# Where the last projection's weight sums are made in a hybrid encoder block

## The chip, the cores and the metric

The kernel runs on one core of a Trainium2 chip. The metric is device time in microseconds (us), the median of several executions. Five engines have instruction queues of their own, and each works its queue in order: PE (TensorE, matrix products), DVE (VectorE), ACT (ScalarE), POOL (GpSimd) and SP (SyncE, which here only issues transfers, DMAs, between the main memory and the memory on the chip). They wait for one another by semaphores. PE writes into PSUM, a small memory of banks that DVE and ACT read out.

## The reference

One layer of a hybrid encoder over 512 frames of 1024 features, all in float32:

```
xn = rmsnorm(x);  u = xn @ w_in            # q | k | v | rnn_x | rnn_gate | gate_A | gate_B
ya = chunked_band_attention(q, k, v) @ w_attn_out
xc = causal_depthwise_conv(rnn_x)          # width 4
hr = rg_lru(xc, ...)                       # 16 diagonal gate blocks, then a scan over time
yb = (hr * gelu(rnn_gate)) @ w_rnn_out
h  = x + (sigmoid(gate_A) * ya + sigmoid(gate_B) * yb) @ w_o
g, up = split(rmsnorm(h) @ w_ffn_in)
out = rmsnorm(h + (silu(g) * up) @ w_ffn_out)
```

The last projection, `w_ffn_out`, has 2816 x 1024 weights. Eleven blocks of 256 rows make it up. Three of them (0, 1, 10) are multiplied plainly; the other eight form four units of two blocks, each multiplied by a Strassen-like scheme: 7 products in place of 8, of sums of the blocks. The sums of the weights (t1 to t4 of a unit) depend on nothing but the weights.

## The kernel before

Activations lie feature by feature or frame by frame in tiles of 128 partitions. Every float32 product is made of three reduced products (`mm3`, L76 to L78): operand and weight are split into a high part (ACT casts, L82) and a low part (DVE subtracts, L83). Weights come in halves of 512 KB: SP issues the load of a `raw` tile (three buffers), ACT and DVE split it into a `whl` tile (four buffers), PE reads that. `weights(name, ahead)` fetches ahead in a fixed list of chunks.

The stages that matter here, in the order of time:

1. The recurrent stage (about 37 to 163 us): a loop over j = 0, 2, 4, 6. For each of two columns c it projects `xr` and makes the convolution (`rnn_conv`: ACT, then three taps on DVE at L495, then the cast and split of `xch` on ACT and POOL), projects `gr` and makes GeLU of it on ACT and DVE, then makes the gates (`rnn_gates`: six small matmuls at L516 into the PSUM tile `rg`, of which there is one buffer, read by four ACT instructions at L520 and L521). From the gates come `u` and `a` (ACT L525 and L526 with the small vectors `sp2` and `spm4`, DVE L528 and L532, POOL L530). After each second j a square root on ACT (L554), then DVE's L537, the scan over time (L538), L539. Last the loop projects `gb`. Below, rg5, xc5 and so on stand for the tile of j = 5.
2. The recurrent way out: the values of the attention's first group (`v_tile(0, t)`), then `yb`, eight columns.
3. Attention, 16 heads, with other projections between; PE's order there is written out by hand.
4. The attention's way out: `ya`, eight columns, then `w_o`.
5. The feed-forward part and the last projection.

Where no order is written out, a scheduler sets the order of each engine's queue at build time, by its own estimate of when each instruction could start. `sp2` and `spm4` come from `softplus_neg` (L436 to L466), a chain of small DVE operations on the tile `sp_p` that the scheduler puts between others.

`spill(u, rooms)` makes the four sums of unit u: four loads of 512 KB from `w_ffn_out` into four buffers, four subtractions on DVE (L749 to L752, each reading the results of those ahead), four stores of 512 KB into a tile `sums` in main memory. The last stage loads the sums from there (L929). Before the change unit 0 is called ahead of `v_tile(0, 0)`, unit 1 at `yb` column 2, units 2 and 3 at `ya` columns 1 and 4. The rooms are tiles of attention (`pt`) and of the values (`v`) that are free at that time.

Of the kernel before, what the change touches and what calls it, by code (L numbers as in the profile page):

```python
# [8 lines left out]
F32 = mybir.dt.float32  # L9
# [5 lines left out]
P = 128  # L15
D = 1024
S = 512
# [19 lines left out]
def block_kernel(ctx: ExitStack, tc: tile.TileContext, x, norm_mix_g, w_in, b_merge, rel_table,  # L37
# [28 lines left out]
    dr = ctx.enter_context(tc.tile_pool(name="dr", bufs=1, space=bass.MemoryType.DRAM))  # L66
# [63 lines left out]
    front, units = (0, 1, 10), ((2, 3), (4, 5), (6, 7), (8, 9))  # L130
# [254 lines left out]
    _, xnT = features(xnp, "xn", "xnT")  # L385
# [189 lines left out]
    def gate(w, j):  # L575
        po = tile_of(f"g{'ab'[w]}{j - j % 2}", j % 2)
        act.activation((ta, zB)[w][j], po[:], AF.Tanh, bias=hb[:, 16 + 8 * w + j:17 + 8 * w + j], scale=0.5)

    conv = {}
    for j in range(0, KT, 2):  # L580
        for c in range(2):
            conv[j + c] = rnn_conv(j + c, tile_of(f"xr{j}", c, ahead=2))
        for c in range(2):
            po = tile_of(f"gr{j}", c, "mm" if j == 0 else "t")
            conv[j + c] += (rnn_gelu(j + c, po),)
            gates_of(j + c)
        for c in range(2):
            gate(1, j + c)
# [39 lines left out]

    q_tile(0)
    k_tile(0)  # L630
    rw2_stack.close()
    rw_stack.close()
    aw2_stack, aw2 = opened("aw2", 2)
    aw_stack, aw = opened("aw", 2, "right")
# [99 lines left out]
        for n in names.split():  # L734
            kinds[n[0]](int(n[1:]))

    sums_d = [[dr.tile([P, 2, S], F32, name=f"sums{u}_{n}") for n in range(4)] for u in range(len(units))]

    def fo_block(i, cc):
        rows = w_ffn_out[2 * P * i:2 * P * (i + 1), cc * S:(cc + 1) * S]  # L740
        return rows.rearrange("(k p) e -> p k e", p=P)

    def spill(u, rooms):

        r = [pl.tile([P, 2, S], F32, tag=tag, bufs=bufs, name=f"spill{u}_{n}") for n, (pl, tag, bufs) in enumerate(rooms)]
        for n in range(4):
            sp.dma_start(out=r[n][:], in_=fo_block(units[u][n // 2], n % 2))
        b11, b12, b21, b22 = (t[:] for t in r)
        dve.tensor_sub(b11, b12, b11)  # L749
        dve.tensor_sub(b12, b22, b12)  # L750
        dve.tensor_sub(b22, b22, b11)
        dve.tensor_sub(b21, b21, b22)  # L752
        for n, i in enumerate((0, 3, 1, 2)):
            sp.dma_start(out=sums_d[u][n][:], in_=r[i][:])

    spill(0, [(aw2, "pt", 4)] * 4)
    for t in range(NT):
        v_tile(0, t)

    for j in range(KT):  # L760
        if j == 6:
            prob = scores(0)
        if j == 2:
            spill(1, [(aw2, "pt", 4)] * 4)
        po = mm_tile(f"po_yb{j}")
        project(po, weights(f"yb{j - j % 2}"), j % 2, rnn)
        dve.scalar_tensor_tensor(zB[j], zB[j], 1.0, po[:], ALU.add, ALU.mult)
# [14 lines left out]

    _, mT = features(xnp, "xn", "mT")
    for j in range(KT):
        if j in (1, 4):
            spill(2 + j // 4, [(aw, "v", 8)] * 4)
        py = mm_tile(f"po_ya{j}")
        project(py, weights(f"ya{j - j % 2}"), j % 2, aT)
        dve.scalar_tensor_tensor(ta[j], ta[j], 1.0, py[:], ALU.add, ALU.mult)
        dve.tensor_add(ta[j], ta[j], zB[j])  # L790
        split_pair(mT[j], ta[j])
# [129 lines left out]
    rooms = [(wp, "whl", 4)]  # L921
# [19 lines left out]
    for j in range(2, FT, 2):  # L941
# [4 lines left out]
        g, u = (sc.tile([P, 4, 256], F32, tag=f"c{w}", name=f"c_{w}{j}") for w in "gu")  # L946
# [201 lines left out]
```

## Time and profile before

| what | us |
|---|---|
| median of 3 runs | 866.72 (866.55 to 866.92) |
| the profiled execution's own time | 866.45 |
| its span, first to last instruction | 864.6 |
| PE busy | 852.5 (99%) |
| DVE busy | 603.5 (70%) |
| ACT busy | 499.4 (58%) |
| POOL busy | 96.7 (11%) |

The granted clock of TensorE was 0.998 over the span. An engine's busy time is the sum of what it worked, not what it held up; a wait shows as idle time before an instruction, with the instruction that ended it. In the views each instruction has its line in the kernel, its engine, what it writes and reads, its shape, its start and its length; L82 is line 82. Matmuls overlap in the records: an instruction of 0.39 us starts every 0.22 to 0.23 us.

### The profile page before, as it was taken

What the parts mean: (1) busy time and instruction counts of PE and PEld (TensorE: products, weight loads), DVE (VectorE), ACT (ScalarE), POOL (GpSimd) and SP (SyncE); (2) the same over time, 40 slices, a digit from 0 to 9 for tenths busy, and PEclk for the clock granted to TensorE, in tenths of its full rate; (3) what the DMA queues carried; (4) which work ended last, traced back from release to release, by engine and by line L of the source; (5) the groups of instructions that cost most, each with busy time, mean ns of one, the idle gap of its engine ahead of it and who ended that gap; (6) DMA issues with size and microseconds to landing.
All of it is one profiled execution on the core that took longest, in us unless ns stands there. A gap on an engine that the chain in (4) does not pass through costs nothing.

```text
span 864.6 us, 12947 instructions
## 1 busy us (share of the span) xinstructions
PE 852.5 (99%) x4920; PEld 747.7 (86%) x4920; DVE 603.5 (70%) x929; ACT 499.4 (58%) x862; POOL 96.7 (11%) x135
## 2 busy tenths in 40 slices
PE   8999999999999999999999999999999999999996
PEld 6977887888888888888888889999999999988885
DVE  5786776674566656566568556888887887399973
ACT  7687687542366656576623365655655556374544
POOL 2022212210113313223200000000000001000011
PEclk9999999999999999999999999999999999999999
DMA  8223324585442213232197811433433333295602
GB/s 271 87 89 96 97 76 122 205 304 184 130 127 73 74 49 110 74 110 75 54 315 264 288 53 49 129 116 98 128 101 115 99 99 98 79 327 159 193 22 97
DMA packets 91901, 113.13 MB, mean 131 GB/s; under 512 B 6080, under 2 KB 71216, under 8 KB 91840
## 3 DMA queue, kind: packets, MB, share of 16 engines
q1 hardware_dynamic: 88160, 104.65, 37.8%
q10 hardware_dynamic: 3680, 7.67, 3.0%
q8 instruction: 38, 0.62, 0.3%
q14 instruction: 23, 0.19, 0.1%
HBM read 101.78 MB, written 10.53 MB: 130 GB/s over the span
## 4 chain that ended last, share of the span: by engine, by line
PE 97%; ACT 1%; DVE 1%; DMA 1%; issue 0%; SPq 0%; DVEq 0%; ACTq 0%
PE po_out L76 4%; PE po_out L77 4%; PE po_out L78 4%; PE p_fg L76 2%; PE o L711 2%; PE p_fg L78 2%; PE p_fu L78 2%; PE p_fg L77 2%; PE p_fu L77 2%; PE p_fu L76 2%; PE pT L691 2%; PE po_gb L77 2%; PE po_gb L76 2%; PE po_ga L76 2%; PE po_v L76 2%; PE po_ga L78 2%
## 5 line engine op out<-in xcount | busy, mean ns | idle before, releaser
L680 POOL TENSOR_SCALAR p<-p,rl 128x128 f32<-128x128 f32 (+1 forms) x64 | 39.6, 637 | 160.6 <-DVE rl L678 160.5
L677 ACT ACTIVATE p<-p,m 128x128 f32<-128x128 f32 (+1 forms) x64 | 35.8, 562 | 12.7 <-DVE m L676 12.7
L918 POOL TENSOR_TENSOR act_lo<-act,act_hi 128x1024 fp32r<-128x1024 f32 x1 | 2.4, 2412 | 298.6 <-ACT act_hi L917 298.6
L83 DVE TENSOR_TENSOR pp<-pT,pp 128x384 fp32r<-128x384 f32 (+1 forms) x48 | 27.8, 596 | 9.8 <-ACT pp L82 9.7
L83 DVE TENSOR_TENSOR whl_qk<-raw_qk,whl_qk 128x1024 fp32r<-128x1024 f32 x16 | 21.5, 1346 | 14.4 <-ACT whl_qk L82 14.3
L676 DVE CUSTOM_DVE_ANT_0 p<-s,bias 128x128 f32<-128x128 f32 (+1 forms) x64 | 29.2, 483 | 2.1 <-PE s L673 2.0
L83 DVE TENSOR_TENSOR whl_fg_s<-s_fg,whl_fg_s 128x1024 fp32r<-128x1024 f32 x20 | 25.6, 1291 | 5.0 <-ACT whl_fg_s L82 5.0
L76 PE MATMUL po_gr<-xnT,whl_gr 128*128 128x512 f32 (+1 forms) x80 | 28.1, 352 | 0.1
L77 PE MATMUL po_xr<-xnT,whl_xr 128*128 128x512 f32 (+1 forms) x80 | 27.9, 354 | 0.0
L77 PE MATMUL po_gr<-xnT,whl_gr 128*128 128x512 f32 (+1 forms) x80 | 27.8, 348 | 0.0
L83 DVE TENSOR_TENSOR whl_fu_s<-s_fu,whl_fu_s 128x1024 fp32r<-128x1024 f32 x20 | 24.0, 1221 | 5.1 <-ACT whl_fu_s L82 5.1
L78 PE MATMUL po_gr<-xnT,whl_gr 128*128 128x512 f32 (+1 forms) x80 | 27.5, 348 | 0.0
L78 PE MATMUL po_xr<-xnT,whl_xr 128*128 128x512 f32 (+1 forms) x80 | 27.3, 346 | 0.0
L76 PE MATMUL po_xr<-xnT,whl_xr 128*128 128x512 f32 (+1 forms) x80 | 26.6, 351 | 0.6 <-ACT xnT L363 0.6
L82 ACT ACTIVATE whl_fg_s<-s_fg 128x1024 fp32r<-128x1024 f32 x20 | 20.9, 1054 | 10.5 <-PE q_fg L78 5.5
L82 ACT ACTIVATE whl_qk<-raw_qk 128x1024 fp32r<-128x1024 f32 x16 | 16.8, 1051 | 16.2 <-PE po_yb L78 8.8
L76 PE MATMUL po_gb<-xnT,whl_gb 128*128 128x512 f32 x64 | 25.2, 393 | 0.3 <-DVE sp_p L455 0.3
L76 PE MATMUL po_ga<-xnT,whl_ga 128*128 128x512 f32 x64 | 25.3, 395 | 0.0
L77 PE MATMUL po_gb<-xnT,whl_gb 128*128 128x512 f32 x64 | 25.3, 395 | 0.0
L76 PE MATMUL po_q<-xnT,whl_qk 128*128 128x512 f32 x64 | 25.0, 391 | 0.0
L78 PE MATMUL po_ga<-xnT,whl_ga 128*128 128x512 f32 x64 | 25.0, 391 | 0.0
L76 PE MATMUL po_k<-xnT,whl_qk 128*128 128x512 f32 x64 | 25.0, 390 | 0.0
(380 smaller groups left out, 3213.4 us busy)
## 6 DMA issues: line engine op xcount, KB each, us to landing
raw_fg<-in_w_ffn_in_dram SPq DMA_DIRECT2D x24, 512.0 KB, 4.6
raw_fu<-in_w_ffn_in_dram SPq DMA_DIRECT2D x22, 512.0 KB, 4.0
raw_qk<-in_w_in_dram SPq DMA_DIRECT2D x32, 256.0 KB, 3.2
spill<-in_w_ffn_out_dram SPq DMA_DIRECT2D x16, 512.0 KB, 7.2
sums<-spill SPq DMA_DIRECT2D x16, 512.0 KB, 3.9
raw_t<-sums SPq DMA_DIRECT2D x16, 512.0 KB, 4.7
raw_b<-in_w_ffn_out_dram SPq DMA_DIRECT2D x12, 512.0 KB, 4.4
raw_xr<-in_w_in_dram SPq DMA_DIRECT2D x8, 512.0 KB, 4.7
```

What stands on the lines that cost most here:

```text
L76: pe.matmul(o, sh, mh, start=start, stop=False, skip_group_check=parts)
L77: pe.matmul(o, sh, ml, start=False, stop=False, skip_group_check=parts)
L78: pe.matmul(o, sl, mh, start=False, stop=stop, skip_group_check=parts)
L82: act.activation(hi, src, AF.Copy)
L83: dve.tensor_sub(lo, src, f(hi))
L676: dve.tensor_tensor_reduce(prob[qb][:], scs[qb], bias[:, S - w:S], -1.0, 3e38, ALU.add, ALU.min, nmax[:, qb:qb + 1])
L677: act.activation(prob[qb][:], prob[qb][:], AF.Exp, bias=nmax[:, qb:qb + 1], scale=-1.0, accum_out=lsum[:, qb:qb + 1])
L680: pool.tensor_scalar(prob[qb][:], prob[qb][:], rl[:, qb:qb + 1], 1.0, ALU.mult, ALU.mult)
L691: pe.transpose(pt[:, at * P:(at + 1) * P], prob[qb][:, kb * P:(kb + 1) * P], ident[:])
L711: pe.matmul(po[:, S - n:S], st, pp[i][:, part, lo:lo + n], start=kb == 0 and part == 0, stop=kb == NT - 1 and part == 1)
L918: (pool if i == 0 else dve).tensor_sub(lo[:], o[:], f(hi[:]))
```

## The change

The calls of `spill` are moved. Units 0, 1 and 2 are made in the recurrent stage, at the head of j = 2, 4 and 6, in four buffers of their own (a pool `early`, which is closed at the end of the stage). Unit 3 is made at `yb` column 3. No call is left in the attention's way out. The helpers move up in the file, so later lines have other numbers.

```diff
+    sums_d = [[dr.tile([P, 2, S], F32, name=f"sums{u}_{n}") for n in range(4)] for u in range(len(units))]
+    def spill(u, rooms):
+        r = [pl.tile([P, 2, S], F32, tag=tag, bufs=bufs, name=f"spill{u}_{n}") for n, (pl, tag, bufs) in enumerate(rooms)]
+        for n in range(4):
+            sp.dma_start(out=r[n][:], in_=fo_block(units[u][n // 2], n % 2))
+        b11, b12, b21, b22 = (t[:] for t in r)
+        dve.tensor_sub(b11, b12, b11)
+        dve.tensor_sub(b12, b22, b12)
+        dve.tensor_sub(b22, b22, b11)
+        dve.tensor_sub(b21, b21, b22)
+        for n, i in enumerate((0, 3, 1, 2)):
+            sp.dma_start(out=sums_d[u][n][:], in_=r[i][:])
+
+    early_stack, early = opened("early", 4)
+
     conv = {}
     for j in range(0, KT, 2):
+        if j >= 2:
+            spill(j // 2 - 1, [(early, "spill", 4)] * 4)
         for c in range(2):
             conv[j + c] = rnn_conv(j + c, tile_of(f"xr{j}", c, ahead=2))
...
     k_tile(0)
+    early_stack.close()
     rw2_stack.close()
...
-    spill(0, [(aw2, "pt", 4)] * 4)
     for t in range(NT):
         v_tile(0, t)
     for j in range(KT):
         if j == 6:
             prob = scores(0)
-        if j == 2:
-            spill(1, [(aw2, "pt", 4)] * 4)
+        if j == 3:
+            spill(3, [(aw2, "pt", 4)] * 4)
         po = mm_tile(f"po_yb{j}")
...
     for j in range(KT):
-        if j in (1, 4):
-            spill(2 + j // 4, [(aw, "v", 8)] * 4)
         py = mm_tile(f"po_ya{j}")
```

The scheduler spreads the new instructions over the stage: units 0 and 1 start in the queues beside the work of j = 0 and 1, so all three units stand between the first column's convolution and that of j = 4. Three places show it. Names end in the buffer's number.

The first is DVE's queue where `sp2` and `spm4` end. Before:

```order
L456 TENSOR_TENSOR sp_p_407<-sp_p_407,sp_s2_405 128x8
L457 TENSOR_SCALAR sp_p_407<-sp_p_407 128x8
L458 TENSOR_TENSOR sp_p_407<-sp_p_407,sp_s_403 128x8
L533 SCALAR_TENSOR_TENSOR gt0_1_556<-gt0_1_556,xc0_476 128x512
L461 SCALAR_TENSOR_TENSOR sp_n_424<-sp_p_407,sp_n_424 128x8
L463 TENSOR_SCALAR sp2_427<-sp_n_424 128x8
L465 TENSOR_SCALAR spm4_429<-sp_n_424 128x8
```

The same chain in the changed kernel:

```order
L456 TENSOR_TENSOR sp_p_407<-sp_p_407,sp_s2_405 128x8
L591 TENSOR_TENSOR spill1_0_997<-spill1_1_998,spill1_0_997 128x1024
L457 TENSOR_SCALAR sp_p_407<-sp_p_407 128x8
L458 TENSOR_TENSOR sp_p_407<-sp_p_407,sp_s_403 128x8
L461 SCALAR_TENSOR_TENSOR sp_n_424<-sp_p_407,sp_n_424 128x8
L463 TENSOR_SCALAR sp2_427<-sp_n_424 128x8
L465 TENSOR_SCALAR spm4_429<-sp_n_424 128x8
L533 SCALAR_TENSOR_TENSOR gt1_1_628<-gt1_1_628,xc1_527 128x512
L495 SCALAR_TENSOR_TENSOR xc2_775<-po_xr2_0_750,vc_383,xc2_775 128x511
```

The first subtraction of unit 1 (L591) has come into the chain, five rows ahead of `sp2`, and the first tap of xc2 now follows that chain.

The second is DVE's queue around the taps of xc4 and xc5. Before:

```order
L538 SCALAR_TENSOR_TENSOR u2_827<-a2_831,gt2_1_822 128x512
L538 SCALAR_TENSOR_TENSOR u2_827<-a3_884,gt3_1_876 128x512
L539 SCALAR_TENSOR_TENSOR u2_827<-u2_827,g2_806 128x512
L539 SCALAR_TENSOR_TENSOR u2_827<-u2_827,g3_860 128x512
L495 SCALAR_TENSOR_TENSOR xc4_1007<-po_xr4_0_982,vc_383,xc4_1007 128x511
L495 SCALAR_TENSOR_TENSOR xc4_1007<-po_xr4_0_982,vc_383,xc4_1007 128x510
L495 SCALAR_TENSOR_TENSOR xc4_1007<-po_xr4_0_982,vc_383,xc4_1007 128x509
L83 TENSOR_TENSOR whl_gb4_0_974<-raw_gb4_0_972,whl_gb4_0_974 128x1024
L83 TENSOR_TENSOR whl_gb4_4_979<-raw_gb4_4_977,whl_gb4_4_979 128x1024
L495 SCALAR_TENSOR_TENSOR xc5_1040<-po_xr4_1_1015,vc_383,xc5_1040 128x511
L495 SCALAR_TENSOR_TENSOR xc5_1040<-po_xr4_1_1015,vc_383,xc5_1040 128x510
L495 SCALAR_TENSOR_TENSOR xc5_1040<-po_xr4_1_1015,vc_383,xc5_1040 128x509
```

In the changed kernel, the last twelve rows up to the same tap:

```order
L537 SCALAR_TENSOR_TENSOR gt2_1_857<-gt2_1_857,u2_862 128x512
L537 SCALAR_TENSOR_TENSOR gt3_1_911<-gt3_1_911,u2_862 128x512
L495 SCALAR_TENSOR_TENSOR xc4_1058<-po_xr4_0_1033,vc_383,xc4_1058 128x509
L538 SCALAR_TENSOR_TENSOR u2_862<-a2_866,gt2_1_857 128x512
L538 SCALAR_TENSOR_TENSOR u2_862<-a3_919,gt3_1_911 128x512
L83 TENSOR_TENSOR whl_gb4_0_1025<-raw_gb4_0_1023,whl_gb4_0_1025 128x1024
L539 SCALAR_TENSOR_TENSOR u2_862<-u2_862,g2_841 128x512
L539 SCALAR_TENSOR_TENSOR u2_862<-u2_862,g3_895 128x512
L83 TENSOR_TENSOR whl_gb4_4_1030<-raw_gb4_4_1028,whl_gb4_4_1030 128x1024
L495 SCALAR_TENSOR_TENSOR xc5_1091<-po_xr4_1_1066,vc_383,xc5_1091 128x511
L495 SCALAR_TENSOR_TENSOR xc5_1091<-po_xr4_1_1066,vc_383,xc5_1091 128x510
L495 SCALAR_TENSOR_TENSOR xc5_1091<-po_xr4_1_1066,vc_383,xc5_1091 128x509
```

The scans and L539 of the pair before, which stood ahead of the taps of xc4, now stand between them and those of xc5. From the first tap of xc2 to the third of xc5 there are 53 rows now (46 without the seven subtractions of units 1 and 2 among them). On PE the gate block rg5 has ten matmuls of gb4 ahead of it where it had seven, and rg1 stands eight matmuls later.

The third is SP's queue from the second half of gr2 on. Before:

```order
L150 DMA raw_gr2_4_700<-in_w_in_dram 128x4x256
L150 DMA raw_gb2_0_705<-in_w_in_dram 128x4x256
L150 DMA raw_gb2_4_710<-in_w_in_dram 128x4x256
L150 DMA raw_xr4_0_900<-in_w_in_dram 128x4x256
L150 DMA raw_xr4_4_905<-in_w_in_dram 128x4x256
```

In the changed kernel:

```order
L150 DMA raw_gr2_4_735<-in_w_in_dram 128x4x256
L596 DMA sums0_0_442<-spill0_0_714 128x1024
L150 DMA raw_gb2_0_740<-in_w_in_dram 128x4x256
L596 DMA sums0_2_444<-spill0_1_715 128x1024
L596 DMA sums0_1_443<-spill0_3_717 128x1024
L589 DMA spill1_0_997<-in_w_ffn_out_dram 128x2x512
L589 DMA spill1_1_998<-in_w_ffn_out_dram 128x2x512
L596 DMA sums0_3_445<-spill0_2_716 128x1024
L589 DMA spill1_2_999<-in_w_ffn_out_dram 128x2x512
L150 DMA raw_gb2_4_745<-in_w_in_dram 128x4x256
L150 DMA raw_xr4_0_935<-in_w_in_dram 128x4x256
L596 DMA sums1_0_446<-spill1_0_997 128x1024
```

The weight loads now stand behind stores that wait for subtractions, and behind loads of the next unit that wait until a store has freed their buffer.

More of the change, by code (lines that the diff above doesn't have):

```diff
@@ L577, in gate, with fo_block @@
         act.activation((ta, zB)[w][j], po[:], AF.Tanh, bias=hb[:, 16 + 8 * w + j:17 + 8 * w + j], scale=0.5)
+    sums_d = [[dr.tile([P, 2, S], F32, name=f"sums{u}_{n}") for n in range(4)] for u in range(len(units))]
+    def fo_block(i, cc):
+        rows = w_ffn_out[2 * P * i:2 * P * (i + 1), cc * S:(cc + 1) * S]
+        return rows.rearrange("(k p) e -> p k e", p=P)
+    def spill(u, rooms):
[10 more added lines that the diff above has]
+    early_stack, early = opened("early", 4)
     conv = {}
     for j in range(0, KT, 2):
+        if j >= 2:
+            spill(j // 2 - 1, [(early, "spill", 4)] * 4)
         for c in range(2):
@@ L735, in project_all @@
             kinds[n[0]](int(n[1:]))
[L737 to L754, printed above, removed]
-    spill(0, [(aw2, "pt", 4)] * 4)
     for t in range(NT):
```

## The prediction, made before the change was run

> **What bounds the kernel now.** I read the page first, for the engine that sets the end.
>
> ```profile
> span 864.6 us, 12947 instructions
> PE 852.5 (99%) x4920; PEld 747.7 (86%) x4920; DVE 603.5 (70%) x929; ACT 499.4 (58%) x862; POOL 96.7 (11%) x135
> PE 97%; ACT 1%; DVE 1%; DMA 1%; issue 0%; SPq 0%; DVEq 0%; ACTq 0%
> ```
>
> PE is busy 99% of the span and holds 97% of the chain that ended last. A busy PE could still hide waits, so the second view is the list of PE's own waits, over the whole span (five rows) and from 60 to 850 us (one row):
>
> ```profile
> PE pt_mix L359 <- DVE xs_mix L351: 1.8, 2, 1.1
> PE busy L309 <- DVE eps_t L315: 1.2, 1, 1.2
> PE po_xr L76 <- ACT xnT L363: 0.6, 2, 0.4
> PE p_fg L76 <- ACT keepa_fg L283: 0.5, 1, 0.5
> PE po_gb L76 <- DVE sp_p L455: 0.3, 1, 0.3
> ```
>
> The third view takes the stages that the change touches: three windows of the recurrent stage, its way out, the attention's way out. The columns are length, then busy time and instructions of PE, PEld, DVE, ACT, POOL, then clock, DMA share and GB/s.
>
> ```profile
> 37.00:67.00 30.00, 29.67 (x136) 23.46 (x135) 26.06 (x45) 22.29 (x30) 6.05 (x5) 1.00 0.35 106
> 67.00:97.00 30.00, 30.00 (x137) 23.75 (x136) 22.11 (x29) 23.68 (x32) 6.79 (x7) 1.00 0.29 88
> 97.00:127.00 30.00, 30.00 (x136) 23.79 (x135) 20.28 (x24) 23.49 (x30) 5.27 (x5) 1.00 0.24 73
> 157.00:190.00 33.00, 33.00 (x149) 27.44 (x149) 22.66 (x30) 16.52 (x26) 6.45 (x4) 1.00 0.79 276
> 432.00:478.00 46.00, 46.00 (x205) 38.11 (x205) 36.22 (x43) 15.91 (x20) 0.00 (x0) 1.00 0.82 287
> ```
>
> So the work leaves places where PE never waits, and goes to a place where PE does not wait yet but DVE is already busy 26 of 30 us. Gain is bounded by PE's waits after 37 us, 0.5 + 0.3 = 0.8 us; loss is not bounded so.
>
> **What leaves, at nothing.** Each unit is four loads, four subtractions and four stores. From the attention's way out go eight subtractions (8 x 1.22 = 9.8 us of DVE), eight loads, eight stores; from the recurrent way out one unit. PE is busy 46.00 of 46.00 and 33.00 of 33.00 us there, so they were hidden under its matmuls and their leaving gives it 0.0. The unit that now stands at j = 3 of the recurrent way out lies under the same cover as the one it replaces, and no unit runs into another there any more: 0.0.
>
> **What comes: twelve subtractions in the recurrent stage.** Their prices, and their DMAs' (issue to landing, min/median/max: the first row of the loads, the second of the stores):
>
> ```profile
> L749 DVE TENSOR_TENSOR spill<-spill,spill x4: 1225/1226/1227, 169.5 to 453.4; 128x1024 f32<-128x1024 f32 x4
> DMA to landing us min/median/max: 2.7/4.3/7.9
> DMA to landing us min/median/max: 2.7/4.1/5.2
> 179.07 4.92 SPq L747 DMA_DIRECT2D spill<-in_w_ffn_out_dram  x3
> 184.92 1.23 DVE L749 TENSOR_TENSOR spill<-spill,spill 128x1024 f32<-128x1024 f32 x1 [4.86 <-DMA spill<-in_w_ffn_out_dram]
> ```
>
> The last two rows are the second unit running into the first: three loads issued from 179.07 on, and DVE stood 4.86 us until they had landed. Twelve x 1.23 = 14.8 us of DVE. That alone costs PE nothing; the question is which instruction in DVE's queue PE waits for, and how late it may be. The tightest I find is the gate block rg5 (L516, for j = 5). It needs PSUM that ACT reads out for rg4, and on ACT those reads stand behind the cast of xch5, which waits for DVE's third conv tap of xc5:
>
> ```profile
> 101.08 2.31 DVE L495 SCALAR_TENSOR_TENSOR xc<-po_xr,vc,xc 128x511 f32<-128x511 f32 x3
> 103.47 0.63 ACT L497 ACTIVATE xch<-xc 128x512 fp32r<-128x512 f32 x1 [3.82 <-DVE xc L495]
> 104.61 1.28 ACT L520 ACT_TABLE_LOAD   x1
> 108.01 0.68 ACT L521 ACTIVATE gt<-rg,hb 64x512 f32<-64x512 f32 x1
> 109.00 0.39 PE L76 MATMUL po_gb<-xnT,whl_gb 128*128 128x512 f32 x1
> 110.68 0.96 PE L516 MATMUL rg<-xch,wrg 64*128 64x512 f32 x6
> ```
>
> The tap ends at 103.39, the reads at 108.69: 5.30 us later. PE comes at 110.68. In the changed order three more matmuls stand ahead of rg5, at 0.22 us each (136 in 30.00 us in the windows), so PE comes at 111.34. **The tap may end at 111.34 - 5.30 = 106.0, which is 2.7 us later than before; what is later still stalls PE one for one.** Four steps give its time.
>
> *Step 1, sp2.* ACT's first tanh of u (L525) needs sp2, the end of a chain of tiny DVE operations:
>
> ```profile
> 44.04 0.73 DVE L495 SCALAR_TENSOR_TENSOR xc<-po_xr,vc,xc 128x509 f32<-128x509 f32 x1
> 49.24 0.17 DVE L463 TENSOR_SCALAR sp<-sp_n 128x8 f32<-128x8 f32 x1
> 49.59 0.82 ACT L525 ACTIVATE u<-gt,sp 128x512 f32<-128x512 f32 x1 [0.33 <-DVE spm L465]
> 54.86 0.68 ACT L521 ACTIVATE gt<-rg,hb 64x512 f32<-64x512 f32 x1
> 57.14 0.76 ACT L493 ACTIVATE xc<-po_xr,vc 128x512 f32<-128x512 f32 x1
> 57.94 0.75 DVE L495 SCALAR_TENSOR_TENSOR xc<-po_xr,vc,xc 128x511 f32<-128x511 f32 x1
> ```
>
> Now the first subtraction of unit 1 stands inside that chain, ahead of sp2. It needs a load into a buffer whose store must land first, and that store follows the second subtraction of unit 0. That subtraction stands just ahead of the tap that began at 44.04; with one more ahead of it, it ends at 44.04 + 2 x 1.2 = 46.4. Store 4.1, load 4.3: 54.8; with 5.8 for the load (issued 179.07 in the crowded place of before, its subtraction at 184.92) 56.3. Subtraction 1.2 and four tiny ones 0.9: sp2 at 56.9 to 58.4, for 49.4 before.
>
> *Step 2, ACT.* rg1 stands eight matmuls later (1.8 us), so its reads end at 55.54 + 1.8 = 57.4 and the tanh starts there at the earliest, or at sp2: 57.4 to 58.5. Two tanh (0.77 each, start to start) and the conv's 0.76: the first tap of xc2 starts at 59.7 to 60.9 (57.94 before). I take 60.3.
>
> *Step 3, DVE's queue to the tap.* From that tap to the third of xc5 stand 53 operations: 12 taps, 22 others of 128x512, 8 weight splits, 4 scans, 7 subtractions. Start to start, from rows like these:
>
> ```profile
> 91.57 2.33 DVE L538 TENSOR_TENSOR_SCAN u<-a,gt 128x512 f32<-128x512 f32 x2
> 93.82 1.27 DVE L539 SCALAR_TENSOR_TENSOR u<-u,g 128x512 f32<-128x512 f32 x2
> 95.00 2.31 DVE L495 SCALAR_TENSOR_TENSOR xc<-po_xr,vc,xc 128x511 f32<-128x511 f32 x3
> 63.16 2.31 DVE L538 TENSOR_TENSOR_SCAN u<-a,gt 128x512 f32<-128x512 f32 x1
> 76.97 1.53 DVE L83 TENSOR_TENSOR whl_xr<-raw_xr,whl_xr 128x1024 fp32r<-128x1024 f32 x1 [0.92 <-ACT whl_xr L82]
> 97.23 3.92 DVE L83 TENSOR_TENSOR whl_gb<-raw_gb,whl_gb 128x1024 fp32r<-128x1024 f32 x2
> 95.29 2.55 POOL L544 TENSOR_TENSOR rnn<-u,rnn 128x512 fp32r<-128x512 f32 x2 [7.33 <-ACT rnn L543]
> 98.17 1.90 POOL L498 TENSOR_TENSOR xch<-xc,xch 128x512 fp32r<-128x512 f32 x1 [0.33 <-ACT xch L497]
> DVE u L532 <- POOL a L530: 1.6, 2, 0.8
> ```
>
> 12 x 0.74 + 22 x 0.60 + 8 x 1.13 + 4 x 1.13 + 7 x 1.14 = 8.9 + 13.2 + 9.0 + 4.5 + 8.0 = 43.6 us, if it never waits (an operation starts 0.08 before the end of the one ahead, as the scans' 2.33 and the 2.25 to the next start show; so a split or a subtraction of 1.22 counts 1.13 or 1.14). The two splits at 97.23 took 3.92 and not 2 x 1.22, because POOL worked on rnn and xch beside them; such excesses between 57.9 and 103.4 sum to 2.9 us in the trace (1.5 here, 1.1 at the scan of 63.16, 0.3 at the split of 76.97), and the same five POOL operations fall into the stretch now. One wait for POOL's a, 0.8. The load for unit 2's second subtraction waits for unit 1's last store: by the same sums it lands within 0 to 1 us after DVE gets there, I take 0.5.
>
> The Trainium skill, SBUF — State Buffer, section "Who interferes with whom", states the rule: a DVE instruction with two SBUF inputs and a GpSimd instruction that reads SBUF exclude each other, and the later one is blocked for the whole of the other. The trace agrees in kind (3.92 for 2.44); taken at its hardest, five POOL operations of 1.29 each block DVE whole, 6.5 us for my 2.9, and an estimate by it would be a stall of 5.7 us. Its 872.1 falls among the third case's times below. I stay with the rows, since operations that start apart block in part.
>
> *Step 4, the sum.* 60.3 + 43.6 + 2.9 + 0.8 + 0.5 = 108.1 for the tap, 2.1 us past the 106.0 that it may take, so PE stalls **2.1 us**. The low end is 59.7 + 43.6 = 103.3, no stall (DVE's idle time swallows all). The high end takes the late start, both POOL waits and one longest load (7.9 for 4.3): 60.9 + 43.6 + 2.9 + 1.6 + 4.1 = 113.1, a stall of 7.1. I take the middle: after the first tap DVE has nothing to wait for but POOL and one load, so little idle time is left.
>
> **Other edits at nothing, and their cover.** SP's queue carries the weight loads behind stores that wait for subtractions and loads that wait for stores; raw_gb2's second half, for one, now stands behind such a load and is issued later. Cover: before, the splits of gb ended at 97.23 + 3.92 = 101.15 and PE first read gb at 109.00, 7.9 us of slack. If an SP wait ate it, PE would stall by what exceeds 7.9. The gate blocks 1 to 4 come out 0.5 to 3 us ahead of PE by the same sums; rg4 is the nearest, but its stall would be part of rg5's, not added. After rg5 no subtraction stands in DVE's queue until the way out, and PE itself is 2 us later, so the loss is paid once.
>
> **The sum.** 866.45 (profiled execution; its span is 864.6) + 2.1 = 868.55. The median of the runs, 866.72, is 0.27 above that execution, so 868.8 on the median's scale. 0.2% is 1.7 us, about what a measurement of this kernel tells from no change.
>
> **Rivals.**
> - *DVE's slack swallows it* (no difference): the tap ends by 107.7. For: before, the same 46 operations took 45.5 us from 57.94 to 103.39 though they need 35.6, so 9.9 us were idle and seven subtractions need 8.0. Against: that idle time was waiting for ACT and PE, and sp2's lateness moves the whole chain. Time 866.7 to 868.4. Chance 0.42.
> - *Forecast, a stall at rg4 and rg5 of 1.7 to 5 us*: 868.4 to 871.7. Chance 0.43.
> - *SP's queue becomes the bound*: three units run into one another, each link a store and a load. If the loads take 7.9 instead of 4.3, two links in a row cost 7.2 us; the weights' cover of 7.9 and the tap's 2.7 are then gone together and the stall is 5 to 9 us: 872 to 876. For: 4.86 us at the one place where two units met. Against: DMA share is 0.24 to 0.35 there, 0.79 at that place. Chance 0.11.
> - *Faster*: the relief of both ways out shows. It would need a wait of PE there, and the view has none: at most 0.8 us, 865.9, which no measurement tells from no change. Beyond 0.2% it needs something that the profile does not show. Chance 0.04.
>
> Faster 0.04, same 0.42, slower 0.43 + 0.11 = 0.54. The range, 866.2 to 871.6, leaves out most of the third case, half of the fourth and little else; the forecast's own is 868.4 to 871.6.
>
> **What would show it.** In PE's waits of the changed kernel a row of L516 with rg, 1 to 4 us, ended by ACT gt (or POOL xch), near 111 us; sp2 near 58 and not 49; DVE busy nearly without gaps from 60 to 108; PE still without a wait in both ways out; the place of rg6 and all behind it moved by the stall. Wrong if PE has no wait at rg5 (then step 3's waits or step 1's landing were too dear), or if the wait stands at a weight split (then SP's queue is the cause).

## The result

| | before | after |
|---|---|---|
| median of the runs, us | 866.63 (866.49 to 868.32, 6 runs) | 872.59 (870.86 to 873.62, 6 runs) |
| the profiled execution, us | 866.45 | 872.1 |
| its span, us | 864.6 | 870.0 |

The ratio of after to before is 1.0064, 95% interval 1.0051 to 1.0077: slower, as forecast (868.8), but by 6.0 us where I had said 2.1, and outside my range (866.2 to 871.6). A second series of the changed kernel, told below, gave 1.0046 (1.0029 to 1.0063).

The spans of the profiled executions differ by 5.4 us. PE's own waits in the changed kernel give the places (us in total, times, longest us):

```profile
PE rg L516 <- issue: 2.3, 1, 2.3
PE pt_mix L359 <- DVE xs_mix L351: 1.6, 2, 1.1
PE po_v L76 <- DVE v L83: 1.4, 1, 1.4
PE rg L516 <- POOL xch L498: 1.2, 1, 1.2
PE po_gb L76 <- ACT zb L577: 0.2, 1, 0.2
```

Three waits are new, and a small one of 0.2: rg5 from 112.8 us (the row that says "issue"), rg3 from 83.0 us, the values' projection po_v from 182.4 us. The four sum to 5.1 us. I had forecast the first, with 2.1 us, and neither of the others.

The same four windows as before (the recurrent stage in three pieces, its way out), and the attention's way out as the fifth:

```profile
37.00:67.00 30.00, 29.46 (x135) 23.23 (x134) 27.05 (x45) 20.58 (x29) 6.79 (x5) 1.00 0.76 268
67.00:97.00 30.00, 28.78 (x130) 22.77 (x129) 26.72 (x32) 21.82 (x29) 8.71 (x5) 1.00 0.81 280
97.00:127.00 30.00, 27.73 (x125) 21.93 (x125) 21.88 (x28) 22.90 (x31) 7.25 (x6) 1.00 0.29 88
157.00:190.00 33.00, 31.61 (x142) 26.05 (x141) 20.99 (x28) 17.57 (x27) 7.45 (x7) 1.00 0.59 208
432.00:478.00 46.00, 46.00 (x207) 38.22 (x206) 25.68 (x33) 15.57 (x19) 0.00 (x0) 1.00 0.29 92
```

In the last row DVE has 10.5 us less to do (25.68 for 36.22) and PE's 46.00 are what they were: nothing came back. In the second row POOL's busy time has risen from 6.79 to 8.71 us though it has nothing new to do: its instructions have become longer.

**rg3.** POOL's subtraction for xch3, with DVE's rows beside it (start, length, engine, line; the number in brackets is idle time before, with what ended it):

```profile
79.16 5.01 POOL L498 TENSOR_TENSOR xch<-xc,xch 128x512 fp32r<-128x512 f32 x1 [12.43 <-issue]
79.48 0.68 DVE L533 SCALAR_TENSOR_TENSOR gt<-gt,xc 128x512 f32<-128x512 f32 x1
80.08 1.21 DVE L591 TENSOR_TENSOR spill<-spill,spill 128x1024 f32<-128x1024 f32 x1
81.22 1.22 DVE L83 TENSOR_TENSOR whl_xr<-raw_xr,whl_xr 128x1024 fp32r<-128x1024 f32 x1
82.36 0.68 DVE L528 SCALAR_TENSOR_TENSOR u<-gt,u 128x512 f32<-128x512 f32 x1
82.96 1.27 DVE L505 SCALAR_TENSOR_TENSOR g<-g,po_gr 128x512 f32<-128x512 f32 x2
86.70 1.62 DVE L592 TENSOR_TENSOR spill<-spill,spill 128x1024 f32<-128x1024 f32 x1 [2.47 <-DMA spill<-in_w_ffn_out_dram]
```

The subtraction takes 5.01 us and ends at 84.17; PE gets on at 84.2. DVE runs without a gap from 79.48 to 82.96 in instructions with two inputs from SBUF, one of them (L591) a subtraction of unit 2, and then comes to L505, whose second input is in PSUM; POOL's result comes 1.21 us after that. The last row is the wait for unit 2's load: 2.47 us where I had put 0.5. That load was issued at 80.40 and landed at 86.58, after 6.2 us.

**rg5**, in the order of the prediction's steps:

```profile
57.92 0.17 DVE L463 TENSOR_SCALAR sp<-sp_n 128x8 f32<-128x8 f32 x1
60.40 0.75 DVE L495 SCALAR_TENSOR_TENSOR xc<-po_xr,vc,xc 128x511 f32<-128x511 f32 x1 [1.64 <-ACT xc L493]
100.59 3.39 DVE L538 TENSOR_TENSOR_SCAN u<-a,gt 128x512 f32<-128x512 f32 x2
107.36 2.30 DVE L495 SCALAR_TENSOR_TENSOR xc<-po_xr,vc,xc 128x511 f32<-128x511 f32 x3
110.40 1.28 ACT L520 ACT_TABLE_LOAD   x1
114.33 0.68 ACT L521 ACTIVATE gt<-rg,hb 64x512 f32<-64x512 f32 x1
```

sp2 at 57.92 (forecast 56.9 to 58.4), the first tap of xc2 at 60.40 (60.3), the third tap of xc5 ends at 109.66 (108.1), ACT's reads at 115.01. The tap is 3.7 us past the 106.0 that I had allowed it, and PE has by then lost 1.2 + 0.2 + 2.3 = 3.7 us.

**v.** DVE's rows on the way out, after and then before:

```profile
181.49 1.52 DVE L594 TENSOR_TENSOR spill<-spill,spill 128x1024 f32<-128x1024 f32 x1
183.03 0.69 DVE L83 TENSOR_TENSOR v<-po_v,v 128x512 fp32r<-128x512 f32 x1
183.78 0.49 PE L76 MATMUL po_v<-whl_v,xnT 128*128 128x512 f32 x1 [1.39 <-DVE v L83]
```

```profile
175.87 1.52 DVE L752 TENSOR_TENSOR spill<-spill,spill 128x1024 f32<-128x1024 f32 x1
177.42 0.69 DVE L83 TENSOR_TENSOR v<-po_v,v 128x512 fp32r<-128x512 f32 x1
178.50 0.39 PE L76 MATMUL po_v<-whl_v,xnT 128*128 128x512 f32 x1
```

The split of v frees the PSUM tile that PE writes next. Before, it ended at 178.11 and PE came at 178.50, 0.39 us of slack behind a unit's four subtractions. Now it ends 5.6 us later, and PE would have come 3.7 us later: 5.6 - 3.7 - 0.4 = 1.5 us of wait.

### The profile page after: what moved, and what is told of

Its sections match the earlier page's. It is cut to its first block, busy times and chain, and to the rows that moved or that the text cites. A ratio compares the mean times of both kernels' runs of the same rounds, so it can differ in the third digit from the quotient of the medians.

```text
span 870.0 us, 12950 instructions
## 1 busy us (share of the span) xinstructions
PE 853.0 (98%) x4920; PEld 748.2 (86%) x4920; DVE 604.2 (69%) x929; ACT 499.4 (57%) x862; POOL 100.8 (12%) x135
## 4 chain that ended last, share of the span: by engine, by line
PE 78%; DVE 5%; ACT 3%; issue 1%; DMA 1%; POOL 0%; SPq 0%; DVEq 0%; POOLq 0%; ACTq 0%
PE po_out L76 4%; PE po_out L77 4%; PE po_out L78 4%; PE p_fg L76 2%; PE o L735 2%; PE p_fu L77 2%; PE p_fg L78 2%; PE p_fu L78 2%; PE p_fg L77 2%; PE p_fu L76 2%; PE pT L715 2%; PE po_ga L76 2%; PE po_ga L78 2%; PE po_ya L76 2%; PE po_h L76 2%; PE po_ga L77 2%
## 5 line engine op out<-in xcount | busy, mean ns | idle before, releaser
L76 PE MATMUL po_v<-whl_v,xnT 128*128 128x512 f32 x64 | 24.9, 395 | 1.4 <-DVE v L83 1.4
L76 PE MATMUL po_gb<-xnT,whl_gb 128*128 128x512 f32 x64 | 25.2, 393 | 0.5 <-DVE sp_p L455 0.3
L76 PE MATMUL po_ga<-xnT,whl_ga 128*128 128x512 f32 x64 | 25.3, 396 | 0.0
L77 PE MATMUL po_gb<-xnT,whl_gb 128*128 128x512 f32 x64 | 25.2, 394 | 0.0
L78 PE MATMUL po_gb<-xnT,whl_gb 128*128 128x512 f32 x64 | 25.1, 392 | 0.0
```

The costliest lines, as they stand in the source:

```text
L76: pe.matmul(o, sh, mh, start=start, stop=False, skip_group_check=parts)
L77: pe.matmul(o, sh, ml, start=False, stop=False, skip_group_check=parts)
L78: pe.matmul(o, sl, mh, start=False, stop=stop, skip_group_check=parts)
```

## The experiments

The first column of waits is PE's at the gate blocks (rg), the second at v. The other columns: DVE's waits for a unit's load between 38 and 116 us, the start of the instruction that makes sp2, the end of the third tap of xc5.

| kernel | rg | v | load | sp2 | tap | profiled span | ratio to before |
|---|---|---|---|---|---|---|---|
| before | 0 | 0 | | 49.2 | 103.4 | 864.6 | |
| the change | 3.5 | 1.4 | 3.5 | 57.9 | 109.7 | 870.0 | 1.0064 (1.0051 to 1.0077) |
| transfers alone | 0 | 0 | | 49.1 | 103.2 | 864.9 | 0.9979 (0.9961 to 0.9998) |
| subtractions alone, short series | 0 | 0.8 | 0 | 53.7 | 106.5 | 870.4 | 1.0069 (1.0047 to 1.0090) |
| short series | 2.2 | 1.0 | 2.5 | 52.6 | 107.4 | 868.1 | 1.0032 (1.0011 to 1.0053) |
| short series, eight buffers | 1.1 | 1.1 | 0 | 56.1 | 104.7 | 867.1 | 1.0023 (1.0011 to 1.0036) |
| eight buffers | 2.7 | 2.8 | 0 | 64.6 | 109.5 | 872.6 | 1.0064 (1.0046 to 1.0082) |
| two units | 0.3 | 1.5 | 1.2 | 58.0 | 106.3 | 866.7 | 1.0019 (1.0009 to 1.0029) |
| two and two | 0 | 0 | 1.0 | 57.7 | 106.0 | 867.1 | 1.0015 (1.0005 to 1.0024) |
| unit 3 late | 3.5 | 0 | 2.5 | 57.9 | 109.6 | 870.0 | 1.0038 (1.0018 to 1.0057) |
| way out alone | 0 | 0 | | | | 868.0 | 1.0020 (1.0002 to 1.0038) |
| xch3 on DVE | 1.7 | 2.4 | 2.2 | 59.0 | 109.4 | 871.9 | 1.0033 (1.0022 to 1.0044) |
| the change again | 3.4 | 1.5 | 2.6 | 57.9 | 109.7 | 870.2 | 1.0046 (1.0029 to 1.0063) |

Single executions of one kernel, the kernel before too, lie up to some us apart (31 runs of before beside the first four experiments: median 866.61, 866.21 to 872.62), so the causes below are read from the waits, and the ratios stand beside them. An edit also makes the scheduler set other orders, on PE too: in the short series, for one, rg5 stands some 2 us later in PE's work, so the 106.0 us that the prediction allows the tap holds only for the order of the change.

### Transfers alone

```diff
-        b11, b12, b21, b22 = (t[:] for t in r)
-        dve.tensor_sub(b11, b12, b11)
+        if u == 3:
+            b11, b12, b21, b22 = (t[:] for t in r)
+            dve.tensor_sub(b11, b12, b11)
...
```

> The changed kernel without the twelve subtractions of units 0 to 2 (so their sums are left out: the blocks are stored as loaded); their 12 loads and 12 stores stay at their places in SP's queue, unit 3 stays whole. Theory (DVE's queue): the third tap of xc5 is no later than PE allows, no wait at rg3 and rg5, and DVE brings no lateness to v: 866.4 to 867.4, 1.000 to 1.001. Rival (the transfers themselves, SP's queue or the busier DMA engines, hold weights or PE up): the recurrent stage loses 1.5 to 4 us as before, 869 to 872, 1.003 to 1.006.

Measured: 866.52 us beside 866.61; no wait at the gate blocks or at v. The first two windows of the recurrent stage:

```profile
37.00:67.00 30.00, 29.67 (x135) 23.43 (x135) 26.08 (x44) 22.13 (x30) 6.06 (x5) 1.00 1.00 366
67.00:97.00 30.00, 30.00 (x136) 23.79 (x135) 22.11 (x29) 23.67 (x32) 6.95 (x7) 1.00 0.61 203
```

POOL's row for xch3 in the same kernel:

```profile
75.95 1.30 POOL L498 TENSOR_TENSOR xch<-xc,xch 128x512 fp32r<-128x512 f32 x1 [3.80 <-issue]
```

The DMA engines are busy all of the first 30 us (1.00, 366 GB/s), and PE's, DVE's and ACT's busy times are those of before. So the transfers by themselves, and SP's queue with all its new entries, cost nothing. In this kernel no store waits for a subtraction, so the links between two units are looser than in the change; that these hold no weights up there either is seen in the change's own list of waits, which has no weight in it. POOL's subtraction takes 1.30 us, not 5.01.

### Subtractions alone

```diff
-            spill(j // 2 - 1, [(early, "spill", 4)] * 4)
+            b11, b12, b21, b22 = (t[:] for t in loose)
+            dve.tensor_sub(b11, b12, b11)
...
```

The four blocks in `loose` are loaded once, at j = 2.

> The twelve subtractions alone in the recurrent stage: four blocks are loaded there once, and the subtractions of three units are made on these with nothing stored (their results go nowhere); the shorter series as in the run before; the sums that count are made as in the run of the way out alone (three units at ya columns 0, 2, 5, which cost 3.4 us there after 480 us), unit 3 at yb column 3. Read up to 190 us. Theory (the wait for a load decides): PE 0 to 0.7 us at rg3 and rg5 together, 0 to 0.7 at v. Rival (twelve subtractions on DVE are enough): 1.7 us or more at rg3 and rg5. Profiled span 868 to 869.2 by the first, 870 or more by the second.

Measured: no wait at the gate blocks, 0.8 us at v. Twelve subtractions that wait for nothing do not cost PE anything at the gates. A reservation: without loads the scheduler sets the subtractions at other places in DVE's queue, and PE's order is another (rg2 comes at 75.7 us, in the change at 70.5). The time itself (873.1 us) holds the three units at ya, and more waits behind 480 us than I had expected; it says nothing of the recurrent stage.

### The short series

```diff
-        dve.tensor_scalar(poly[:], s2[:], 1.0 / 17, 1.0 / 15, ALU.mult, ALU.add)
-        for c in (13, 11, 9, 7, 5, 3):
+        dve.tensor_scalar(poly[:], s2[:], 1.0 / 7, 1.0 / 5, ALU.mult, ALU.add)
+        for c in (3,):
```

> The changed kernel with a shorter series in the softplus chain (one pair of the loop in place of six, so terms of the series are left out and ten tiny DVE operations go); sp2 then stands ahead of unit 1's first subtraction. Theory (step 1: that subtraction waits for a store and a load and holds sp2 until 58.1, and with it ACT's tanh and DVE's first work on u): sp2 near 50, DVE makes u of j = 0 before the first tap of xc2 and that tap starts 0.7 us earlier, the third tap of xc5 ends about 2 us earlier (107.5), PE's loss up to rg5 falls from 3.7 to 1 to 2 us: 869.5 to 871, 1.0035 to 1.005. Rival (sp2's place does not matter, the loss is the seven subtractions and the wait for unit 2's load): 872 to 872.6, 1.0065.

Measured: sp2 at 52.6 us, the first tap of xc2 at 58.93 (1.5 earlier), the third tap of xc5 ends at 107.4, as expected; the waits at the gates fall from 3.5 to 2.2 and the profiled span from 870.0 to 868.1. They stand at other blocks, though: 0.5 us at rg3 and 1.7 at rg4, both for POOL's xch, and rg5, which PE reaches at 115.75, waits for nothing. So step 1 of the prediction, sp2 behind a subtraction that waits for data, is a part of the loss, together with the orders that come of it; the edit does not part the two.

> A control: the kernel before with the shorter series (terms of the series left out) and nothing else. Theory: ten tiny DVE operations fewer, in a stage where PE waits for none of them but 0.3 us at po_gb: profiled span 864.3 to 864.8, the kernel before's time within 0.05%. Rival (the shorter series gains something of its own, so that its gain in the changed kernel is not the units'): 865.5 or less.

The control, the same edit in the kernel before: 866.29 beside 866.32, ratio 0.9996 (0.9986 to 1.0005). The series itself gains nothing. Its profiled span is 866.3 (the others 864.3 to 865.0), and most of the 1.7 us lie outside the places of this study: PE waited 0.8 and 0.4 us for weights of `w_o`, in the attention's way out, where the kernel before had no wait in its own profiled execution.

### Eight buffers

```diff
-            spill(j // 2 - 1, [(early, "spill", 4)] * 4)
+            spill(j // 2 - 1, [(early, "spill", 8)] * 4)
```

> As the run with the shorter series (terms of the series left out), with eight buffers in place of four for the units in the recurrent stage, so that the second unit's loads wait for no store. In the run with four, DVE waited 2.5 us for loads of a unit between 38 and 116 us, PE 2.2 us at rg3 and rg5, 1.0 at v. Theory (the wait for a load is the part of the tap's lateness that decides): DVE waits under 1 us for loads, PE 0 to 0.7 us at rg3 and rg5 together and 0 to 0.7 at v: profiled span 864.8 to 866.2. Rival (the subtractions' own time and the blocking with POOL are enough): 1.7 us or more at rg3 and rg5, 867.5 or more.

Measured: DVE waits for no load any more, the tap of xc5 ends at 104.7, and of the short series' two waits at the gates the one at rg4 (1.7 us) is gone. The tap is 2.7 us earlier than with four buffers and the same series (107.4), where the waits for loads were 2.5. The two figures agree, but the orders differ again (the first tap of xc2 comes 0.7 us later here, at 59.66), so this does not show that such a wait goes into the tap one for one. What is left is 1.1 us for POOL's xch3, and 1.1 at v, more than I had expected:

```profile
75.41 5.15 POOL L498 TENSOR_TENSOR xch<-xc,xch 128x512 fp32r<-128x512 f32 x1 [9.42 <-issue]
78.21 1.21 DVE L593 TENSOR_TENSOR spill<-spill,spill 128x1024 f32<-128x1024 f32 x1
79.35 1.27 DVE L505 SCALAR_TENSOR_TENSOR g<-g,po_gr 128x512 f32<-128x512 f32 x2
80.54 1.21 DVE L594 TENSOR_TENSOR spill<-spill,spill 128x1024 f32<-128x1024 f32 x1
```

The pattern of rg3 again: POOL's instruction lasts 5.15 us, until DVE has come to L505 (79.35), and ends 1.21 us after that, at 80.56.

> The changed kernel with eight buffers in place of four for the units in the recurrent stage, the series whole; so the second unit's loads wait for no store, and nothing else is edited. In the change PE waited 3.5 us at rg3 and rg5 together and DVE 2.5 us for a load there; with the shorter series and eight buffers 1.1 and 0. Theory (the wait for a load is the larger part of the loss): no wait of DVE for a load over 1 us, PE 1.0 to 2.0 us at the gate blocks, profiled span 867 to 868.5. Rival (sp2's place is the larger part: with the whole series four more subtractions stand ahead of it): 3 us or more at the gate blocks, 869 or more.

With the whole series and eight buffers DVE waits for no load either, but four subtractions of unit 1 now stand ahead of sp2, which comes at 64.6. PE waits 2.7 us at the gates (all at rg4), 2.8 at v (2.0 for v, 0.8 for its weights): no better than the change, 1.0064. My expectation of 1.0 to 2.0 us was wrong, and the rival's 3 us the nearer. So neither the wait for a load nor sp2's place is the cause alone; with both put right, in the run before, 1.1 us is left at rg3.

### Two units, and two and two

```diff
-        if j >= 2:
-            spill(j // 2 - 1, [(early, "spill", 4)] * 4)
+        if j >= 4:
+            spill(j // 2 - 2, [(early, "spill", 4)] * 4)
...
+        if j == 2:
+            spill(2, [(aw, "v", 8)] * 4)
         py = mm_tile(f"po_ya{j}")
```

> Two units (0 and 1) in the recurrent stage, at the places that the first two of the change have; unit 2 alone in the attention's way out (ya column 2), unit 3 at yb column 3 as changed. Theory (the tap of xc5 is late by the sum of what stands ahead of it on DVE): without unit 2's four subtractions (4 x 1.14 = 4.6 us) and the 2.5 us wait for its load, the tap ends at 104 to 106.3 in place of 109.7 and may end at 106.0; POOL's xch3 isn't locked out for 5 us: PE waits 0 to 0.4 us at rg3 and rg5 together (3.5 in the change) and 0 to 0.5 at v (1.4): profiled span 864.8 to 865.7, 866.6 to 867.6. Rival (sp2's lateness, which the first unit makes, is what costs): a wait at rg5 of 2 us or more, 869 or more.

Measured: the tap ends at 106.33. PE waits 0.3 us at rg3 and not at rg5, which it reaches 0.45 us later than the prediction's 111.34, at 111.79; so the tap was allowed 106.5, and its 106.33 fits the prediction's 106.0. But the 1.5 us at v are as in the change, where I had expected 0 to 0.5. PE is nearly in time here and DVE is not: its row L533 for j = 7 starts 2.6 us later than before (152.74 for 150.16), its split of v still ends 2.4 us later (180.49 for 178.11), PE's rg7 starts 0.4 us later (146.0 for 145.6). 2.4 less 0.4 and less the 0.4 of slack is 1.6, the wait.

The next kernel has the same two units, and units 2 and 3 at ya columns 1 and 4, as before.

> Units 0 and 1 in the recurrent stage, at the places that the first two of the change have, units 2 and 3 in the attention's way out at ya columns 1 and 4, where the kernel before has them; nothing in the recurrent way out. With unit 3 at yb column 3, two units left PE a wait of 0.3 us at rg3 and 1.5 at v. Theory (that 1.5 is unit 3's four subtractions ahead of v, on a DVE that comes late out of the recurrent stage): no wait at v, 0.3 at the gate blocks, profiled span 864.9 to 865.4, 866.5 to 867.1. Rival (DVE's lateness alone is enough): a wait at v of 1 us or more, 867.8 or more.

No wait at v and none of note at the gates; 867.12 us beside 866.32, most runs with spans of 864.7 to 865.2. The profiled one has 867.1, of which 1.6 are waits for the weights of `w_o`, as in the control. It is the fastest version with units in the recurrent stage, and it isn't faster than the kernel before.

### Unit 3 late, and the way out alone

```diff
-        if j == 3:
-            spill(3, [(aw2, "pt", 4)] * 4)
         po = mm_tile(f"po_yb{j}")
...
+        if j == 1:
+            spill(3, [(aw, "v", 8)] * 4)
         py = mm_tile(f"po_ya{j}")
```

> The changed kernel with unit 3 made in the attention's way out (column 1 of ya) in place of the recurrent way out; the recurrent stage is as changed. Theory (the recurrent stage leaves DVE and ACT 5.6 to 5.9 us late and PE only 3.7, and unit 3's four subtractions stand ahead of the split of v that frees PE's PSUM at 182 us): without them the 1.4 us wait of po_v for DVE's v goes, the waits at rg3 and rg5 stay (1.2 and 2.3): 1.4 to 1.5 us less than the change, 871.1, 1.0052 of the kernel before. Rival (DVE's lateness alone holds v up, whatever stands ahead of it): the wait stays, 872.6, 1.0069.

Measured: the wait at v is gone, those at the gates are the same to 0.1 us. The median is 871.8, not 871.1, and the profiled span is 870.0 as with the change. The stretch behind rg5's wait (the column behind POOL's is PE's clock), here and then in the change, has the reason:

```profile
116.50:120.00 3.50, 3.50 (x10) 2.68 (x10) 3.03 (x4) 3.47 (x6) 0.62 (x1) 0.51 0.41 123
```

```profile
116.50:120.00 3.50, 3.50 (x18) 2.85 (x17) 3.02 (x4) 3.47 (x6) 0.63 (x1) 1.00 0.41 125
```

After the same wait of 2.3 us TensorE ran for 3.5 us at half its clock here, 10 matmuls for 18, some 1.7 us. Without it the span would be 868.3, which is what two of the ten runs have.

The way-out part alone:

```diff
-        if j >= 2:
-            spill(j // 2 - 1, [(early, "spill", 4)] * 4)
...
+        if j in (0, 2, 5):
+            spill(j // 2, [(aw, "v", 8)] * 4)
         py = mm_tile(f"po_ya{j}")
```

> Only the way-out part of the change: unit 3 at yb column 3 as changed, units 0, 1 and 2 in the attention's way out (ya columns 0, 2, 5), nothing in the recurrent stage. Theory (the wait at v is lateness brought along from the recurrent stage): no wait of PE at v, rg3 or rg5, 866.3 to 866.9, 1.000 of the kernel before. Rival (unit 3 at that place costs by itself): a wait of about 1.4 us at po_v for DVE's v, 868.0, 1.0017.

No wait at v, rg3 or rg5: unit 3 at its new place costs nothing on a DVE that is in time. The time, 869.66, is not what I expected. From 480 us on, behind the three units at ya, PE waits 1.9 us (p_fg 0.9, q_fg 0.5, po_h 0.5) where the kernel before has 0.5; that is 1.4 of the 3.4 us by which the span is longer, and I haven't placed the rest.

### xch3 on DVE

```diff
-        pool.tensor_sub(xch[:, 1], xc[:], f(xch[:, 0]))
+        (dve if j == 3 else pool).tensor_sub(xch[:, 1], xc[:], f(xch[:, 0]))
```

> The changed kernel with the low part of xch3, one subtraction of 128x512, made by DVE in place of POOL. In the change POOL's took 5.01 us and PE waited 1.2 us for it at rg3. Theory (that wait is not lost twice: PE loses up to rg5 what the tap of xc5 is late, 3.7 us, whatever it waited before): the wait at rg3 goes, the one at rg5 grows from 2.3 to 3.5 or more, and the total stays: profiled span 869.5 to 871. Rival (the lock costs its own 1.2 us): 2.3 at rg5, none at rg3, profiled span 868.8.

Measured: 1.7 us at the gates in all (none at rg3, 1.3 at rg5, 0.3 at rg6), neither my 3.5 nor the rival's 2.3. The whole execution starts 1.1 us later than the change's (sp2 at 59.0), so the tap's 109.4 is 1.4 earlier in its own time. DVE's longest wait for a load is 1.2 us where it was 2.5, because DVE reached it later, having had xch3 to do. But L592 then ends only 0.6 us earlier in its own time (88.79 - 1.09 for 88.32); the rest of the 1.4 comes behind it, in a queue whose order is another (the first tap of xc5 now stands between the two L539). The wait at rg3 is thus not simply handed on to rg5, as I had thought. The wait at v rose to 2.4, and behind it the clock was 0.50 from 186 to 188 us.

This profiled execution is the slowest of eleven (873.74 us). Their median, 870.04, is 2.3 us below that of the change in nine executions (872.32, below), and the ratios, 1.0033 and 1.0046, have intervals that overlap. So the edit probably gains some 2 us; whether the lock at rg3 would cost 1.2 us with everything else held still, this run can't tell.

### The change again

> The changed kernel once more, for a second profiled execution and a narrower ratio. Theory (the waits at the gate blocks follow from the order of DVE's queue and the loads, so they come again; the wait at v holds about 1.1 us that come from one collision of DVE's L539 with POOL's L544 at 133 us, where now DVE and now POOL is first, as 0.69 us of L539 in one run and 1.78 in another show): rg3 and rg5 together 3.0 to 4.0 us; v 1.4 where L539 took 1.8 us, 0.3 to 0.5 where it took 0.7. Where PE's stall at rg5 is followed by half the clock (0.51 over 3.5 us in the run with unit 3 late), 1.6 us more. Rival (the waits of the first profiled execution were its own): 2 us or less at rg3 and rg5.

Measured: 872.32 us, ratio 1.0046 (1.0029 to 1.0063) beside runs of before that spread more than in the other series (median 867.63). The waits are those of the first execution:

```profile
PE rg L516 <- issue: 2.3, 1, 2.3
PE po_v L76 <- DVE v L83: 1.5, 1, 1.5
PE rg L516 <- POOL xch L498: 1.1, 1, 1.1
```

They are the kernel's, not one execution's. L539 took 1.8 us in both, so the second half of that expectation, a shorter wait at v where L539 takes 0.7, had no case here.

What lies behind the wait at rg5 was not quite the same. Here first, then in the first execution:

```profile
85.90 1.86 DVE L592 TENSOR_TENSOR spill<-spill,spill 128x1024 f32<-128x1024 f32 x1 [1.66 <-DMA spill<-in_w_ffn_out_dram]
86.64 1.59 POOL L530 TENSOR_SCALAR a<-u 128x512 f32<-128x512 f32 x1
88.27 0.69 DVE L532 SCALAR_TENSOR_TENSOR u<-u 128x512 f32<-128x512 f32 x1 [0.51 <-POOL a L530]
```

```profile
86.63 0.62 POOL L530 TENSOR_SCALAR a<-u 128x512 f32<-128x512 f32 x1
88.25 0.68 DVE L532 SCALAR_TENSOR_TENSOR u<-u 128x512 f32<-128x512 f32 x1
```

The load landed 5.5 us after its issue in place of 6.2, and DVE waited 1.7 us for it in place of 2.5. The tap ended no earlier (109.69 for 109.66): L592 and POOL's a now met, a took 1.59 us for 0.62, and DVE waited 0.5 us for it. With unit 3 late it was the same (1.5 us for the load, L532 at 88.20, the tap at 109.63). So two things end together at L532, the load and POOL's queue, which ran without a gap from xch3's 5.01 us through rnn to a. A load that lands about 1 us earlier gains nothing; POOL, held up at xch3, is then the one that DVE waits for.

## Why the prediction was right or wrong

**What leaves, at nothing:** right for ya (46.00 of 46.00 in both). In the control PE waited 1.2 us just behind ya, for the weights of `w_o` (486 to 488 us), with the same two units, so the cover is thinner than one profile shows.

**The allowance of 106.0** and **steps 1 and 2** were right: sp2, the first tap of xc2, and the place and sign of rg5's wait. In the change the tap ended 3.7 us past 106.0, and PE had lost 3.7 us by the end of rg5's wait, the 1.2 us at rg3 included.

**Step 3** failed in what DVE waits behind its first tap. From 60.40 to 109.66 are 49.3 us. Waits for loads took 2.5 (I had 0.5), POOL's a 0.8 (0.8), collisions with POOL 2.6 (2.9: L532 1.1, L592 0.4, the scan 1.1), which leaves 43.4 for the operations (43.6). I had let the load land 0 to 1 us after DVE got there, from a median landing of 4.3 us. It landed after 6.2, in a stretch where the DMA share had risen from 0.29 to 0.81; higher prices were in my own quoted rows (7.9 at most; 5.8 us from the first of two loads to their subtraction, at share 0.79). Step 1 used the 5.8, the high end of the range the 7.9, and the forecast here neither. In the second execution the same stretch lost 1.7 for the load, 1.3 for POOL's a and 2.8 in collisions. I had 4.2 us for the three together, the two executions have 5.9 and 5.8, and that is the 1.6 us by which the tap was later than forecast. The load's landing is not the whole of it: POOL, late behind xch3, stands close behind the load, as the second execution shows.

The estimate with five POOL operations that block DVE whole, 872.1, is the profiled execution's time by luck alone: DVE lost 2.6 us to POOL and not 6.5.

**"The gate blocks 1 to 4 come out 0.5 to 3 us ahead of PE"** was wrong at rg3. I had counted what DVE loses to POOL and not what POOL loses to DVE. The Trainium skill, SBUF — State Buffer, section "Who interferes with whom", says that a DVE instruction with two SBUF inputs and a GpSimd instruction that reads SBUF block each other and that issue order decides. It also says that a DVE instruction with one SBUF input doesn't take part; by that, POOL gets in at L505, and 84.17, 80.56 (1.21 us after L505 begins, both times) agree. I took the rule in one direction only. Up to rg5 PE lost no more than the tap was late, so the wait at rg3 lies within the 3.7 us.

**"The loss is paid once"** and **the way-out unit at 0.0** were wrong: 1.4 us of the 5.1, from a term that I had put at nothing. With the 1.6 us of step 3 it takes the time out of the range (868.8 + 1.6 + 1.4 = 871.8); either alone would have left it inside. I named as cover that PE was busy 33.00 of 33.00 us. That says that PE did not wait; it does not say by how much. The slack at v was 0.39 us. And DVE and ACT come out of the recurrent stage later than PE does. In the change DVE's second L539 of that pair begins 4.8 us later than before (132.98 for 128.17), and there it also loses to POOL:

```profile
132.98 1.78 DVE L539 SCALAR_TENSOR_TENSOR u<-u,g 128x512 f32<-128x512 f32 x1
```

```profile
128.17 0.68 DVE L539 SCALAR_TENSOR_TENSOR u<-u,g 128x512 f32<-128x512 f32 x1
```

From there on it is 5.9 us late (134.76 for 128.85), and 5.6 still at v. In the execution with unit 3 late L539 took 0.69. The runs with units 0 to 3 apart (unit 3 late: no wait; the way out alone: no wait; two units and unit 3: 1.5) show that it takes both, a late DVE and the unit ahead of v. How much of the wait the collision at L539 makes is open: with the short series it took 0.68 and v still waited 1.0.

**The rivals.** The time lies in the range of the one that I gave 0.11, SP's queue, but not by its mechanism: no weight split is waited for at the gates, and the transfers alone, all of SP's new entries included, cost nothing. One link of it was true, units running into one another through a store and a load; it stalls DVE, not the weights. In the first rival, "the same 46 operations" is a slip: before, 43 of them stand between the two taps (three of L528 and L532 come earlier), which need 33.8 us at the same prices, so 11.6 us were idle or lost to POOL there and not 9.9. As said there, that time went to waiting for ACT and PE, and the late sp2 moved the chain whole.

So the cause, as far as it is shown: subtractions in an in-order queue that wait for data (1.5 to 2.5 us for unit 2's load), push sp2 back by 8.7 us, and leave DVE so few gaps that POOL's xch waits too; DVE comes out of the stage later than PE, and unit 3 ahead of v makes PE wait once more. Transfers alone cost nothing, subtractions alone nothing at the gates. What each part costs by itself stays open, since nearly every edit also changed the orders of the queues.

## What to carry to other kernels

Before work is moved into a stage, take from the trace not whether the bound engine waits there but by how much its inputs are early, at each hand-over behind the new work; 0.4 us of slack and 10 look the same in a busy share. Price a transfer at its new place by the DMA share that the place will have after the move. And when an engine comes out of a stage late, follow its lateness, not the bound engine's, to the next place where the two meet.

## What the runs showed of the hardware

A waiting POOL instruction was not let in between DVE instructions that follow one another without a gap. Its record lasted 5.01 us (the change), 5.15 (short series, eight buffers), 4.37 (short series) and 3.90 (two units), for 1.30 without the subtractions, over three to five DVE instructions, and ended in all four 1.21 to 1.23 us after DVE had begun one with an input from PSUM (L505). I had thought of the loser as blocked by one instruction.

Which of the two loses does not follow from the starts alone. In the change and in the run with unit 3 late POOL's L544 starts 0.24 us ahead of DVE's second L539 (132.74 and 132.98; 132.71 and 132.95); L539 took 1.78 us in the one and 0.69 in the other.

A wait of PE of 2.3 us can cost more than itself. In the run with unit 3 late it was followed by 3.5 us at a clock of 0.51; the wait of 2.4 us at v in the run with xch3 on DVE by a clock of 0.50, one of 2.7 us at a gate with eight buffers by 0.51 over 3.5 us (107.4 to 110.9). In two executions of the change, after the same 2.3 us, the clock stayed at 1.00. Nor does it take one wait of that length: in the run with xch3 on DVE the clock was 0.50 from 12 to 14 us as well, behind four waits of 0.2 to 1.1 us between 6 and 11 us, and that execution is 1.1 us late from there on. The Trainium skill, TensorE: Matmul & The Clock Gate, section "What's actually happening", has the clock halved after an idle window of about 3.4 us that runs freely; the half clock's length agrees, but the gaps here were shorter than that.
